# Gate and up projections with the tokens stationary and 512 weight columns moving

## The chip, the cores and the metric

The kernel runs on one core of one Trainium2 chip. The metric is the device time of one launch in microseconds. TensorE (PE, with its weight loads as PEld) multiplies, VectorE (DVE) and ScalarE (ACT) work elementwise and read and write PSUM, GpSimd (POOL) adds in SBUF, and SyncE (SP) issues the DMAs. Each engine works its own queue in order.

## The reference, cut to what matters

One layer for 512 tokens of width 2048, all in float32: token mixing, a residual, then the feed-forward part that the change touches.

```python
D_MODEL = 2048; SEQ = 512; D_FF = 5632

x = x + mix @ w_out[l]
h2 = _rms_norm(x, norm2_g[l])
x = x + (jax.nn.silu(h2 @ w_gate[l]) * (h2 @ w_up[l])) @ w_down[l]
```

## The kernel before, in words

**Stages.** Input projection with the two attentions and the convolution beside it (to about 394 us), output projection (to 582 us), gate and up (582 to 1441 us), down (to the end). Everything is emitted in one program order per engine (`manual_schedule`), so the order of the Python calls is the order of each engine's queue.

**Precision.** A float32 operand is split in two `fp32r` parts, a high part (a rounding copy) and a low part (what is left). A product is three matmuls: high by high, high by low, low by high.

**Strassen's scheme.** Gate, up and down are each computed as 2 by 2 block products with seven multiplications instead of eight (Winograd's form). A product is named by a number; `ORDER` (L66) gives the order for gate and up, `D_ORDER` (L76) that of down. The sums of the token operands are made once and kept in `ops[q, j]`, one tile of 128 x 512 for each of 7 products and 8 row pairs: 256 tokens' high parts in columns 0 to 255, their low parts in 256 to 511 (`TH` = 256). The sums of weight blocks are made on POOL (`sums`, called by `sums_now` at the start of a unit).

**Units.** Work on weights goes in units of 128 x 1024 float32. `pump` issues the DMA of a unit's raw block on SP as soon as its buffer was given back (`take`, `drop`), in the order of `entries`. `split_up_to` makes a unit's parts two units ahead (`SPLIT_AHEAD` = 2, three buffers each for `hi` and `lo`): ACT copies the raw block to `near` in PSUM and to `hi`, DVE subtracts `near` from the raw block into `lo`. `near` has two PSUM buffers (pool `high`). Units marked `"moves"` (those of down) have their columns permuted on the way, by the same three instructions (L280 to L282).

**Gate and up before.** There are 44 groups: for each pair `p` of 22 (one 128-row tile from each half of the feed-forward width) a gate group and an up group. A group has seven products, one unit each: `Block.multiply` (L1146) issues 8 matmuls with `wh` stationary and 512 columns moving (256 tokens' high and low parts side by side) and 8 with `wl` stationary and 256 columns moving (high parts). The features lie on the partitions of the result and the tokens on its columns; main and rest halves of a bank are added by DVE (`both`, `add`, `done`). `finish` multiplies by the token scale `R_21` (from `norm2a` and `norm2b`) and applies Silu for gate, and multiplies up by gate. Then `sums1`, `sums2` (POOL) form the operands of down, and `piece1` to `piece4` split them (ACT, DVE) and store them to `od`.

**Down.** `Down.product` (L1345) has the tokens' operands stationary (`acts`, read back from `od` by `load_next`) and 512 columns of `wh` and `wl` moving (L1404 to L1406), two banks, one for each 128 tokens.

**Queues of small work.** `later(n, fn)` puts a call into `evacs` (run at the start of a unit, before its splits are issued) or `extras` (run after its matmuls), n entries on. `done` of a product is run at the start of the unit behind it. Four PSUM banks (`outs`) take turns. `turn_x2` and `turn_x2_now` read the residual from DRAM turned (`z<-x2d`, in pieces of 32 floats), turn its 32 x 32 blocks on DVE and store them for down.

Of the kernel before, what the change touches and what calls it, by code (L numbers as in the profile page):

```python
# [65 lines left out]
ORDER = (5, 1, 7, 6, 2, 4, 3)  # L66
# [5 lines left out]
GU_ORDER = [*range(NP)]  # L72
# [7 lines left out]
LAID = (5, 7, 6, 4, 3, 1, 2)  # L80
# [36 lines left out]
def kernel(ctx: ExitStack, tc: tile.TileContext, xT, wi, wo, wgu, wd, cst_in, outT):  # L117
# [51 lines left out]
    def group(name, m, n, blocks):  # L169

        key = {k: (k, name) for k in ("11", "12", "21", "22", "s")}
        for k in ("22", "21", "11", "12"):
            entries.append((k + "ab"[m] if k[0] == "2" else k, key[k], blocks[k]))
        u = len(works)

        def add(to, a, b, last=None):
            def go():
                if to == a:
                    out = raws[key[to]][0]
                else:  # L180
                    out = take("s" + "ab"[m], key[to], n)
                nc.gpsimd.tensor_add(out[:, :n], raws[key[a]][0][:, :n], raws[key[b]][0][:, :n])  # L182
                if last:
                    drop(key[last])
            return go

        sums[u - 4].append(add("s", "21", "22"))
        sums[u - 3].append(add("21", "21", "11"))
        sums[u].append(add("s", "s", "11", "11"))
        sums[u + 2].append(add("s", "s", "12"))  # L190
        works.extend((key[k], last, None) for k, last in (
            ("s", False), ("11", False), ("21", True), ("s", False), ("12", True), ("22", True), ("s", True)))

    for p in GU_ORDER:
        for m in range(2):
            group(f"{'gu'[m]}{p}", m, 1024, {f"{i + 1}{k + 1}": [wgu[4 * (p + i * NP) + 2 * m + k]]
                                             for i in range(2) for k in range(2)})


    bufs = {"A": dict(zip(("21", "11", "s", "22"), ("21a", "22a", "sa", "22b"))),  # L200
            "B": dict(zip(("21", "11", "s", "22"), ("21b", "11", "12", "sb")))}

# [5 lines left out]
    for t, (g, r) in enumerate(DOWN):  # L208
# [12 lines left out]
        def add(c, out, one, other, buf=None):  # L221
            key, n = keys[c], size[c]

            def go():

                to = take(buf, key[out], n) if buf else raws[key[out]][0]
                nc.gpsimd.tensor_add(to[:, :n], raws[key[one]][0][:, :n], raws[key[other]][0][:, :n])
            return go
# [14 lines left out]
    def pump(limit, most=99):  # L243
        while at["entry"] < len(entries) and len(raws) < limit and entries[at["entry"]][0] not in held and most:
            most -= 1
            buf, key, parts = entries[at["entry"]]
            if len(parts[0].shape) == 3:
                n = 4 * parts[0].shape[-1]
                nc.sync.dma_start(take(buf, key, n)[:, :n].rearrange("p (n f) -> p n f", n=4), parts[0])
                at["entry"] += 1  # L250
                continue
            t, o = take(buf, key, sum(p.shape[-1] for p in parts)), 0
            for part in parts:
                nc.sync.dma_start(t[:, o:o + part.shape[-1]], part)
                o += part.shape[-1]
            at["entry"] += 1
# [830 lines left out]
    r2b = cp.tile([P, 3 * TH], F32, name="r2b")  # L1087
    R_12, R_21, R_1, R_2 = r2b[:, :T], r2b[:, TH:], r2b[:, :TH], r2b[:, TH:T]
# [4 lines left out]
    def norm2a():  # L1093

        n2["r"] = token_scale(ssum2, D, "n2", blk.banks[6][:, :NT])[1]
# [30 lines left out]
    class Block:  # L1126

        def __init__(self, name, m):  # L1130
            self.name = name

            self.banks = dict(zip((5, 1, 7, 6), outs))
            self.banks.update({3: self.banks[5], 4: self.banks[7], 2: self.banks[1]})
            outs[:] = [self.banks[q] for q in (6, 2, 4, 3)]

        def multiply(self, q, w, xs):
            wh, wl = w
            b = self.banks[q]
            at = [(x, slice(j * P, (j + 1) * P)) for j, x in enumerate(xs)]  # L1140

            begin = q in (5, 1, 6, 7)
            for low in ((0, 1) if flip[0] else (1, 0)):
                for x, s in at:
                    out, lhs, rhs = (b[:, TH:], wl, x[:, :TH]) if low else (b, wh, x)
                    nc.tensor.matmul(out, lhs[:, s], rhs, start=begin, stop=x is xs[-1] and low == flip[0],  # L1146
                                     skip_group_check=True)
                    begin = False
            flip[0] = 1 - flip[0]
            later(0, self.done, q)  # L1150

        def both(self, q, out):
            nc.vector.tensor_reduce(out, self.banks[q].rearrange("p (a b) -> p b a", a=2),
                                    axis=mybir.AxisListType.X, op=ALU.add)

        def add(self, q, out, first=None, sign=nc.vector.tensor_add):
            main, rest = halves(self.banks[q])
            sign(out, out if first is None else first, main)
            sign(out, out, rest)

    class Wide(Block):


        def __init__(self, p, m, gate):
            super().__init__(f"{'gu'[m]}{p}", m)
            self.p, self.gate = p, gate

        def done(self, q):
            if q == 1:
                self.u = slot(f"{self.name}u")  # L1170
                self.u1, self.u2 = halves(self.u)
                self.both(1, self.u1)
            elif q == 7:
                self.l, self.r = slot(f"{self.name}l"), slot(f"{self.name}r")
                self.both(7, self.r[:, :TH])
                self.add(5, self.r[:, :TH], sign=nc.vector.tensor_sub)
            elif q == 6:
                self.add(6, self.u2, self.u1)
                nc.gpsimd.tensor_sub(self.r[:, :TH], self.r[:, :TH], self.u2)
            elif q == 2:  # L1180
                self.both(2, self.r[:, TH:])
                self.finish(self.r, self.gate and self.gate.r)
            elif q == 4:
                c21 = self.l[:, TH:]
                main, rest = halves(self.banks[4])
                nc.vector.tensor_sub(c21, main, self.u2)
                nc.vector.tensor_add(c21, c21, rest)
            elif q == 3:
                self.add(3, self.l[:, :TH], self.u2)
                self.u = self.u1 = self.u2 = None  # L1190
                self.finish(self.l, self.gate and self.gate.l)
# [36 lines left out]
        def piece1(self):  # L1228
            self.piece(0, self.ta)
# [321 lines left out]
```

## Time and profile before

| | |
|---|---|
| median of 3 runs | 1867.45 us (1867.01 to 1867.95) |
| profiled execution | 1867.59 us, of which the span is 1865.9 us |
| granted TensorE clock | 1.00 |
| busy share of the span: PE, DVE, ACT, POOL | 100%, 78%, 71%, 61% |
| gate and up stage, by its first and down's first matmul | 581.93 to 1440.61 us |
| bytes moved, mean rate | 307.38 MB, 165 GB/s |

A row of a group names the line, the engine, the operation, output and inputs, shape and count, then busy time, the mean nanoseconds of one, and the idle time before it. In the timeline the first column is the start and the second the length, both in us; matmuls are pipelined, so the distance of two starts and not the length is what a matmul costs.

### The profile page before, as it was taken

The page shows a single profiled execution, that of the slowest core. Times are in us where ns is not written, and L with a number is a line of the kernel's source. Part 1 is how long each engine was busy: PE and PEld are TensorE (multiplying, and loading weights), DVE is VectorE, ACT ScalarE, POOL GpSimd, SP SyncE. Part 2 cuts the span into 40 slices and gives each one's busy share as a digit, 9 for nine tenths or more (in the row PEclk, how much of TensorE's full clock was granted, in tenths as well). Part 3 has the DMA queues.
Part 4 walks back from the last instruction along what each step waited for, and adds up shares of the span by engine and source line. Part 5 has one row for each costly group of instructions (what it writes and reads, how often), then busy time and mean ns, then how long its engine had stood idle before and what let it go on. Part 6 is the DMA issues. An engine that isn't in the chain of part 4 may idle for free.

```text
span 1865.9 us, 28280 instructions
## 1 busy us (share of the span) xinstructions
PE 1858.8 (100%) x9606; PEld 1591.2 (85%) x9606; DVE 1446.7 (78%) x2290; ACT 1330.5 (71%) x1840; POOL 1141.7 (61%) x828
## 2 busy tenths in 40 slices
PE   9999999999999999999999999999999999999998
PEld 7888888888888888888888888888888888888887
DVE  6778878998689777777777777777777777777777
ACT  6355644553457878888888888888888877778775
POOL 0125533100013877888878878788787878779775
PEclk9999999999999999999999999999999999999999
DMA  7243253343333455555555655555457867677645
GB/s 273 77 145 90 77 147 96 94 130 120 131 123 113 146 160 158 174 183 158 174 158 171 186 155 178 159 171 185 143 168 249 315 226 237 210 228 234 203 131 113
DMA packets 213328, 307.38 MB, mean 165 GB/s; under 512 B 75200, under 2 KB 124992, under 8 KB 213184
## 3 DMA queue, kind: packets, MB, share of 16 engines
q1 hardware_dynamic: 213040, 305.57, 52.3%
q8 instruction: 76, 1.25, 0.3%
q14 instruction: 68, 0.56, 0.1%
q10 hardware_dynamic: 144, 0.01, 0.0%
HBM read 244.03 MB, written 53.09 MB: 159 GB/s over the span
## 4 chain that ended last, share of the span: by engine, by line
PE 99%; DMA 0%; SPq 0%; DVE 0%; issue 0%; ACT 0%; DVEq 0%
PE out L1146 46%; PE out L1405 7%; PE out L1404 7%; PE out L1406 7%; PE o L317 3%; PE o L315 3%; PE o L316 3%; PE cq L315 2%; PE cq L317 2%; PE cq L316 2%; PE ak L315 1%; PE aq L315 1%; PE av L315 1%; PE aq L317 1%; PE aq L316 1%; PE av L316 1%
## 5 line engine op out<-in xcount | busy, mean ns | idle before, releaser
L1146 PE MATMUL out<-h,wh 128*128 128x512 f32 x2464 | 588.5, 391 | 0.0
L1146 PEld LDWEIGHTS out<-h,wh 128*128 128x128 f32 x2464 | 452.7, 188 | 87.5
L1146 PEld LDWEIGHTS out<-h,wl 128*128 128x128 f32 x2464 | 315.9, 191 | 12.0
L1146 PE MATMUL out<-h,wl 128*128 128x256 f32 x2464 | 319.6, 283 | 0.0
L1404 PE MATMUL out<-wh,a 128*128 128x512 f32 x620 | 240.4, 388 | 0.0
L1405 PE MATMUL out<-wl,a 128*128 128x512 f32 x620 | 240.3, 388 | 0.0
L1406 PE MATMUL out<-wh,a 128*128 128x512 f32 x620 | 240.3, 388 | 0.0
L286 ACT CAST wh<-w 128x1024 fp32r<-128x1024 f32 (+2 forms) x94 | 96.8, 1031 | 151.0 <-PE o L316 62.8
L264 DVE TENSOR_TENSOR wl<-w,wh 128x1024 fp32r<-128x1024 f32 (+2 forms) x95 | 113.2, 1191 | 41.1 <-ACT wh L286 39.5
L1404 PEld LDWEIGHTS out<-wh,a 128*128 128x128 f32 x620 | 116.4, 188 | 24.0
L1406 PEld LDWEIGHTS out<-wh,a 128*128 128x128 f32 x620 | 116.4, 188 | 23.8
L1405 PEld LDWEIGHTS out<-wl,a 128*128 128x128 f32 x620 | 116.4, 188 | 23.8
L1414 DVE TENSOR_TENSOR y<-y,out 128x512 f32<-128x512 f32 x164 | 106.2, 683 | 25.7 <-PE out L1406 23.8
L526 DVE SCALAR_TENSOR_TENSOR y<-bu,cst,y 128x511 f32<-128x511 f32 (+14 forms) x120 | 90.0, 750 | 0.7
L315 PE MATMUL o<-mh_c,wh 128*128 128x512 f32 x128 | 51.1, 399 | 0.0
L315 PE MATMUL cq<-hh,wh 128*128 128x512 f32 x128 | 50.5, 395 | 0.0
L317 PE MATMUL o<-mh_c,wl 128*128 128x512 f32 x128 | 50.0, 391 | 0.0
L316 PE MATMUL cq<-hl,wh 128*128 128x512 f32 x128 | 49.9, 390 | 0.0
L316 PE MATMUL o<-ml_c,wh 128*128 128x512 f32 x128 | 49.9, 390 | 0.0
L317 PE MATMUL cq<-hh,wl 128*128 128x512 f32 x128 | 49.9, 390 | 0.0
L431 POOL TENSOR_TENSOR lvr<-lvv,nhalf 128x4 f32<-128x4 f32 x1 | 1.9, 1923 | 70.7 <-DVE lvv L430 70.7
L182 POOL TENSOR_TENSOR w('s', 'g0')_5667<-w('21', 'g0')_5513,w('22', 'g0')_5511 128x1024 f32<-128x1024 f32 x1 | 2.5, 2454 | 69.0 <-DVE wl L264 69.0
(3062 smaller groups left out, 4941.6 us busy)
## 6 DMA issues: line engine op xcount, KB each, us to landing
od<-a SPq DMA_DIRECT2D x154, 256.0 KB, 4.7
a<-od SPq DMA_DIRECT2D x154, 256.0 KB, 5.5
w<-in_wi SPq DMA_DIRECT2D x58, 512.0 KB, 3.5
w<-in_wo SPq DMA_DIRECT2D x32, 512.0 KB, 3.5
x<-in_xT SPq DMA_DIRECT2D x16, 256.0 KB, 7.1
xr<-in_xT SPq DMA_DIRECT2D x16, 256.0 KB, 3.8
x2d<-xr SPq DMA_DIRECT2D x16, 256.0 KB, 2.0
z<-x2d SPq DMA_DIRECT2D x64, 64.0 KB, 3.8
```

Of the source, the lines that this page charges most:

```text
L182: nc.gpsimd.tensor_add(out[:, :n], raws[key[a]][0][:, :n], raws[key[b]][0][:, :n])
L264: fn(*args)
L286: (nc.vector.tensor_copy if u == 0 else nc.scalar.copy)(hi[:, :n], t[:, :n])
L315: nc.tensor.matmul(out, wh, xh, start=start, stop=False)
L316: nc.tensor.matmul(out, wh, xl, start=False, stop=False)
L317: nc.tensor.matmul(out, wl, xh, start=False, stop=stop)
L526: nc.vector.scalar_tensor_tensor(yconv[j][:, i:], hconv[j][:, :T - i], c, yconv[j][:, i:], op0=ALU.mult, op1=ALU.add)
L1146: nc.tensor.matmul(out, lhs[:, s], rhs, start=begin, stop=x is xs[-1] and low == flip[0], skip_group_check=True)
L1404: nc.tensor.matmul(b[:, lo:hi], x[:, high], wh[:, s], start=start, stop=False, skip_group_check=True)
L1405: nc.tensor.matmul(b[:, lo:hi], x[:, high], wl[:, s], start=False, stop=False, skip_group_check=True)
L1406: nc.tensor.matmul(b[:, lo:hi], x[:, low], wh[:, s], start=False, stop=last, skip_group_check=True)
L1414: getattr(eng, op)(t, t, src)
```

## The change

For gate and up the operands change places: 128 columns of `ops[q, j]` (128 tokens, high or low parts) become stationary, and 512 columns of `wh` or `wl` move (256 gate or up features from each of two pairs; two row pairs make a unit). A unit is then 12 matmuls of 512 columns, for two banks of 128 tokens. The 44 groups become 11 blocks of two halves (row pairs 0 to 3 and 4 to 7) of seven products of two units: 28 units a block, 308 units as before. The order of the products is new, and so are the weight buffers' turns; each raw block is read in two parts, in pieces of 1 KB instead of 4 KB.

Tokens lie on the partitions of the result. The first half's results are copied out of PSUM (`keep`, one bank on ACT, one on DVE), the others are added to them (`add`); the corrections by product 6 run on POOL. The token scale is now a per-partition scalar of Silu and of the multiplication `weigh`, so that the spread of the scale over the partitions goes. The result is turned to features on partitions: DVE turns 32 x 32 blocks (`turn`), `store` writes them to a tile in DRAM, and `Pair.read` reads them back, each time four DMAs of 32 partitions in pieces of 32 floats. `Pair` then makes the operands of down as before: sums on POOL, splits on ACT and DVE, stores to `od`. In the last block's second half two loads of down's operands are issued a unit (28 in all), where before three were in the last group (21 in all).

```diff
-ORDER = (5, 1, 7, 6, 2, 4, 3)
+ORDER = (7, 1, 4, 2, 5, 6, 3)
...
+def up_block(pair, m, half, j):
+    return [bass.AP(tensor=wgu.tensor, offset=wgu.offset + (4 * (pair + i * NP) + 2 * m + half) * P * 1024 + j * P,
+                    ap=[[1024, P], [4 * P * 1024, 2], [1, 2 * P]]) for i in range(2)]
...
+    for i, c in enumerate("AB"):
+        key = keys[c]
+        sums[base - 4 + i].append(plus(key["s"], key["21"], key["11"], 1024, bufs[c]["s"]))
+        sums[base + 2 + i].append(plus(key["21"], key["21"], key["22"], 1024))
+        sums[base + 6 + i].append(plus(key["11"], key["21"], key["11"], 1024))
+        sums[base + 7 + i].append(plus(key["12"], key["11"], key["12"], 1024))
+    works.extend((keys[c][k], last, "moves") for k, last in (
+        ("s", True), ("11", False), ("22", True), ("12", False), ("21", True), ("11", True), ("12", True)) for c in "AB")
...
-    def norm2b():
-        b = psum["high"].tile([P, 1024], F32, name="r2s", tag="h")[:, :T]
-        spread(n2["r"], "r2s", b)
-        nc.scalar.copy(R_12, b)
-        nc.scalar.copy(r2b[:, T:], b[:, :TH])
+    def norm2():
+        b = psum["high"].tile([P, 1024], F32, name="r2s", tag="h")[:, :NT]
+        n2["r"] = token_scale(ssum2, D, "n2", b)[1]
...
+    class Pair:
+        def __init__(self, dram, p, n):
+            for at, fn in ((0, self.read_l), (1, self.read_r), (4, self.sums), (5, self.piece_r), (7, self.piece_l),
+                           (8, self.sum4), (9, self.piece_a), (11, self.piece_4)):
+                later(at, fn, queue=extras)
+        def read(self, n, name):
+            t = slot(f"p{self.p}{name}")
+            for part in range(4):
+                at = (4 * n + part) * 32
+                nc.sync.dma_start(t[32 * part:32 * part + 32].rearrange("p (x i) -> p x i", i=32),
+                                  self.dram.rearrange("(x j) f -> j x f", j=32)[:, :, at:at + 32])
...
+        def sums(self):
+            nc.gpsimd.tensor_sub(n1, c11, c12)
+            nc.gpsimd.tensor_sub(c12, c12, c22)
+            nc.gpsimd.tensor_sub(n2, c12, c11)
...
+    class Up:
+        def product(self, q):
+            banks = outs[:2]
+            outs[:] = outs[2:] + banks
+            for c in range(2):
+                sums_now()
+                run(evacs)
+                wh, wl = next_unit()
+                for a, b in enumerate(banks):
+                    high, low = slice(a * P, (a + 1) * P), slice(TH + a * P, TH + (a + 1) * P)
+                    for f in range(2):
+                        x, s = ops[q, self.first + 2 * c + f], slice(f * T, (f + 1) * T)
+                        nc.tensor.matmul(b, x[:, high], wh[:, s], ...)
+                        nc.tensor.matmul(b, x[:, high], wl[:, s], ...)
+                        nc.tensor.matmul(b, x[:, low], wh[:, s], ...)
+                yield
+                run(extras)
+            later(0, self.done, self.first == 0, q, banks)
...
+        def done(self, first, q, banks):
...
+            if q == 6:
+                u = [self.c.pop((2, 0, a)) for a in range(2)]
+                for a in range(2):
+                    self.add(1, 0, a, u[a], nc.gpsimd, "tensor_sub")
+                for a in range(2):
+                    if first:
+                        self.c[0, 1, a] = u[a]
+                    else:
+                        self.add(0, 1, a, u[a], nc.gpsimd)
+                for a in range(2):
+                    self.add(1, 1, a, u[a], nc.gpsimd, "tensor_sub")
+            if not first and q in (2, 3):
...
+                later(0, self.gate, k, queue=extras)
+                at = 1 if k else 6
+                later(at, self.weigh, k)
+                later(at + 1, self.turn, k)
+                later(at + 2, self.store, k, queue=extras)
+            if not first and q == 3:
+                later(5, Pair, self.dram, 2 * self.n, 0, queue=extras)
+                later(15, Pair, self.dram, 2 * self.n + 1, 1, queue=extras)
...
-    for g in range(2 * NP):
-        p, m = GU_ORDER[g // 2], g % 2
-        blk = Wide(p, m, gate if m else None)
...
+    for n in range(NBLOCKS):
+        blk = Up(n)
+        for blk.first in (0, 4):
+            for i, q in enumerate(ORDER):
+                for c, _ in enumerate(blk.product(q)):
+                    at_unit = (7 if blk.first else 0) * 2 + 2 * i + c
+                    if n == 0 and at_unit == 2:
+                        norm2()
+                    if 1 <= n <= 8 and at_unit in (9, 12, 25, 27):
+                        (turn_x2 if at_unit % 16 == 9 else turn_x2_now)(SUMS[2 * n - 2 + at_unit // 16])
+                    if n == NBLOCKS - 1 and blk.first:
+                        load_next(2)
```

More of the change, by code (lines that the diff above doesn't have):

```diff
@@ L71 @@
 FEED = 46
-GU_ORDER = [*range(NP)]
+NBLOCKS = NP // 2
 D_ORDER = (7, 1, 5, 6, 4, 2, 3)
@@ L167 @@
         works.append((u, True, nc.vector))
[L169 to L192, printed above, removed]
@@ L221, in add @@
         def add(c, out, one, other, buf=None):
[L222 to L228, printed above, removed]
+            return plus(keys[c][out], keys[c][one], keys[c][other], size[c], buf)
         for i, c in enumerate("AB"):
@@ L246, in pump @@
             buf, key, parts = entries[at["entry"]]
[L247 to L255, printed above, removed]
+            size = [part.shape[-1] * (part.shape[1] if len(part.shape) == 3 else 1) for part in parts]
+            t, o = take(buf, key, sum(size)), 0
+            for part, n in zip(parts, size):
+                to = t[:, o:o + n]
+                nc.sync.dma_start(to.rearrange("p (n f) -> p n f", n=part.shape[1]) if len(part.shape) == 3 else to, part)
+                o += n
             at["entry"] += 1
@@ L1124, in later @@
         queue[n].append((fn, *args))
[L1126 to L1159, printed above, removed]
@@ L1459, in done @@
                     later(2 * n + 2, put, self.g, i, k, queue=extras)
-    blk = gate = None
     for t in range(len(DOWN)):
```

190 lines of the change are left out of this document (99 added, 91 removed).

## The prediction

> **What bounds the kernel now.** I read the page's busy shares and the chain of waits first, then TensorE's timeline in the two stages that use the two arrangements, then the other engines by stage.
>
> ```profile
> PE 1858.8 (100%) x9606; PEld 1591.2 (85%) x9606; DVE 1446.7 (78%) x2290; ACT 1330.5 (71%) x1840; POOL 1141.7 (61%) x828
> PEclk9999999999999999999999999999999999999999
> PE out L1146 46%; PE out L1405 7%; PE out L1404 7%; PE out L1406 7%; PE o L317 3%; PE o L315 3%; PE o L316 3%; PE cq L315 2%; PE cq L317 2%; PE cq L316 2%; PE ak L315 1%; PE aq L315 1%; PE av L315 1%; PE aq L317 1%; PE aq L316 1%; PE av L316 1%
> ```
>
> TensorE is busy for the whole span at full clock, and the chain that ends last is matmuls, 46% of it on L1146, the one line of gate and up. A busy PE need not be PE at its peak, so I look at the distance of the starts.
>
> ```profile
> 904.37 3.82 PE L1146 MATMUL out<-h,wh 128*128 128x512 f32 x16
> 908.02 2.08 PE L1146 MATMUL out<-h,wl 128*128 128x256 f32 x16
> 909.93 3.82 PE L1146 MATMUL out<-h,wh 128*128 128x512 f32 x16
> 913.59 2.08 PE L1146 MATMUL out<-h,wl 128*128 128x256 f32 x16
> 915.50 0.86 PE L1146 MATMUL out<-h,wh 128*128 128x512 f32 x3
> ...
> 1699.69 0.39 PE L1404 MATMUL out<-wh,a 128*128 128x512 f32 x1
> ...
> 1705.81 0.39 PE L1404 MATMUL out<-wh,a 128*128 128x512 f32 x1
> ```
>
> In gate and up, four units take 915.50 - 904.37 = 11.13 us, 2.7825 us a unit. Sixteen matmuls of 512 columns take 908.02 - 904.37 = 3.65 us (228.1 ns each), sixteen of 256 columns 909.93 - 908.02 = 1.91 us (119.4 ns): half the columns cost more than half the time. In down, with the tokens stationary and 512 columns moving, the 27 steps from the first to the last row shown (the rows left out are the matmuls between, one a step) take 6.12 us, 226.7 ns each. No wait shows between them.
>
> ```profile
> 581.93 1.98 PE L1146 MATMUL out<-h,wh 128*128 128x512 f32 x8
> 587.50 0.95 PE L358 MATMUL out<-ones,ssum 128*128 128x1 f32 x8
> 588.31 2.11 PE L1146 MATMUL out<-h,wh 128*128 128x512 f32 x8
> 594.01 0.60 PE L364 MATMUL r2s<-ident,n2r 128*128 128x128 f32 x4
> 594.36 2.09 PE L1146 MATMUL out<-h,wh 128*128 128x512 f32 x8
> 1440.61 0.39 PE L1404 MATMUL out<-wh,a 128*128 128x512 f32 x1
> ```
>
> The stage lasts 1440.61 - 581.93 = 858.68 us: 308 units of 2.7825 us are 857.0, the row sums of the norm (587.50 to 588.31) 0.81, the spread of the scale (594.01 to 594.36) 0.35, together 858.2. So the stage is TensorE's own pace, with half a microsecond of anything else.
>
> **The change, part by part.**
>
> *TensorE.* A unit becomes 12 matmuls of 512 columns. At down's 226.7 ns that is 2.720 us, 308 units 837.9 us; the row sums stay (0.81), the spread goes. 838.7 against 858.7: **-20.0 us**. The other bound is 512 columns at the 228.1 ns of the old stage: 2.737 us a unit, 843.0 + 0.8, -14.9 us. I take down's value, since its operands, order and accumulation are the new ones.
>
> [...]
>
> *Is there cover for the rest?* All other work must fit beside 2.720 us units, on engines that were this busy before:
>
> ```profile
> 900.00:1000.00 100.00, 100.00 (x577) 88.40 (x576) 76.63 (x114) 83.25 (x108) 80.63 (x52) 1.00 0.55 171
> ...
> L281 ACT CAST wh<-w('11', 'd0A')_14861 x3: 1055/1057/1057, 1440.9 to 1468.0; 128x1024 fp32r<-128x1024 f32 x3
> L280 ACT CAST wn<-w('11', 'd0A')_14861 x3: 1007/1010/1022, 1438.1 to 1466.4; 128x1024 fp32r<-128x1024 f32 x3
> L282 DVE TENSOR_TENSOR wl<-w('11', 'd1A')_15411,wn x3: 1214/1215/1222, 1479.5 to 1506.7; 128x1024 fp32r<-128x1024 f32 x3
> L1414 DVE TENSOR_TENSOR y<-y,out x164: 648/682/689, 1445.8 to 1849.4; 128x512 f32<-128x512 f32 x164
> L1424 ACT COPY d0u<-out x2: 581/585/589, 1451.1 to 1451.7; 128x512 f32<-128x512 f32 x2
> L1267 DVE STREAM_TRANSPOSE zt<-z x16: 703/704/705, 714.0 to 1298.5; 128x512 f32<-128x512 f32 x16
> L526 DVE SCALAR_TENSOR_TENSOR y<-bu,cst,y x120: 693/732/941, 62.7 to 460.4; 128x511 f32<-128x511 f32 x4, 128x510 f32<-128x510 f32 x4, 128x509 f32<-128x509 f32 x4, 128x508 f32<-128x508 f32 x4
> L1225 DVE TENSOR_TENSOR a<-u0r,u0n x2: 412/413/414, 626.5 to 626.8; 128x256 fp32r<-128x256 f32 x2
> L1414 POOL TENSOR_TENSOR y<-y,d0u x8: 1282/1300/1309, 1453.2 to 1488.0; 128x512 f32<-128x512 f32 x8
> L1208 POOL TENSOR_TENSOR u0ta<-u0r,u0l x1: 742/742/742, 624.9 to 624.9; 128x256 f32<-128x256 f32 x1
> 901.84 2.42 POOL L182 TENSOR_TENSOR w('s', 'u8')_9381<-w('21', 'u8')_9193,w('22', 'u8')_9191 128x1024 f32<-128x1024 f32 x1
> ```
>
> The first row is a window of the old stage: DVE, ACT and POOL 77, 83 and 81% busy, the DMA engines 55%. For a new block of 28 units (76.2 us):
> - DVE: 28 low parts at 1.215, 18 sums and 5 copies out of PSUM at 0.68, 4 multiplications at 0.73, 4 turns at 0.70, 14 splits at 0.41, some 2 turns of the residual: 62.6 us, 82%.
> - ACT: the splits stay (28 times 1.01 + 1.06), Silu and the splits of down's operands stay, 5 copies at 0.59 come: 2.9 us, +4%, and the unit is 2% shorter: about 89%.
> - POOL: 16 weight sums at 2.42, 10 corrections at 1.30, 8 sums at 0.74: 57.6 us, 76%.
>
> On average all fit. What counts is where the work piles up.
>
> *The start.*
>
> ```profile
> 588.22 0.42 DVE L1043 TENSOR_TENSOR h<-h,h 128x256 fp32r<-128x256 f32 x1
> 588.56 1.21 DVE L264 TENSOR_TENSOR wl<-w('21', 'g0')_5513,wn 128x1024 fp32r<-128x1024 f32 x1
> ```
>
> DVE makes the last token operands until 588.6. (Two neighbours of 0.42 us start 0.34 us apart: lengths overlap.) The third unit's low part, which stood behind them, is now issued with its split, ahead of them; so they end at 589.8, and the fourth unit's low part at 591.0, due at 581.93 + 3 x 2.72 + 0.23 = 590.3: **+0.7 us** (0 to 2). The token operands of rows 4 to 7 aren't needed before unit 14, so none of them is late.
>
> *The turn of a block*, the worst place, on DVE. Call 0 the start of the next block's first unit. The corrections by product 6 start on POOL when DVE has summed it, at -5.44 + 2 x 0.68 = -4.1; the fourth ends at +1.1. DVE's second sum of product 3 waits for it and ends at 1.8. Then, in queue order: the low part of unit 2 to 3.0 (due with that unit's second matmul, 5.7), two `weigh` to 4.5, unit 3 to 5.7 (due 8.4), two turns to 7.1, two `weigh` to 8.5, a copy to 9.2, unit 4 to 10.4 (due 11.1), two turns to 11.8, unit 5 to 13.0 (due 13.8). So 13 us of work go through a stretch of 10.9 us, and being two units ahead saves it by 0.7 us. I price it at 0 inside the stage, with 1.3 us a block as the other end (POOL 2 us behind at that point).
>
> *The hand-over to down* is that turn with four sums of product 7 in place of one copy: 3 x 0.68 = 2.0 us more against 0.7 us of room, and less than that, since neighbours overlap, as in the row pair above. I take **+0.8 us** (0 to 2).
>
> *SP and the turned reads.* A block adds 4 stores and 16 reads (some 0.5 us of SP each) and 16 weight DMAs, and the reads wait on SP for the stores to land. Behind them in SP's queue stand weight blocks, issued 10 us and more ahead of their use.
>
> ```profile
> 933.95 2.02 SPq L1263 DMA_DIRECT2D z<-x2d  x4
> L1263 SPq DMA_DIRECT2D z<-x2d x64: 369/487/1132, 700.2 to 1286.2; - x64
> DMA to landing us min/median/max: 3.3/3.8/5.2
> 934.00:939.00 5.00, 5.00 (x31) 4.43 (x31) 3.86 (x6) 4.70 (x7) 3.31 (x4) 1.00 0.69 157
> 1440.00:1500.00 60.00, 60.00 (x267) 49.67 (x266) 44.82 (x57) 49.10 (x59) 48.63 (x29) 1.00 0.90 318
> ```
>
> The read of the residual has the same shape and pieces: issue 2 us for four, 3.8 us (3.3 to 5.2) to landing. The next row is the stretch in which one set and one weight block (512 KB) moved: 0.69 x 5.0 = 3.5 us of all DMA engines, of which the block is 1.5 us at the rate of the last row, 318 / 0.90 = 353 GB/s. So a set (256 KB) costs some 2.0 us, four sets and four stores (0.75 us each) a block 11 us of 76: the DMA share goes from 0.55 to about 0.7. Enough is left; I price it at 0.
>
> **Sum** against the profiled execution (span 1865.9 us, its own time 1867.59, 0.14 above the median): -20.0 + 0.8 + 0.7 = -18.5 us. 1867.45 - 18.5 = **1849.0 us**, -1.0%. The likeliest case's own range is 1845.5 (no stall, and 1 us less than the sum) to 1854 (the 228.1 ns bound).
>
> **The rivals.**
>
> *DVE is late at every turn* (chance 0.15). For it: the 0.7 us of room, and that DVE there waits for POOL, which stands behind 2.42 us sums. Against it: that overlap, which I left out of the 13 us. Each 1 us beyond the room costs 11 us: at 0.4 to 1.3 us a block 1853 to 1863.
>
> *The turned reads land late, and POOL stands still* (chance 0.18, slower). In the second half of a block, `Pair.sums` stands in POOL's queue ahead of three weight sums. The read can be issued some 12 us into that half (behind a weight block that waits for unit 5's split) and lands at 16 to 18. From there two sums (1.5 us), two weight sums (4.8), a split (1.0 + 1.2) must be done by 30.1, when unit 11 starts: the read has until 21.6. Landing 3.6 us later than I assume, it costs 11 us for each further us; from 1.7 us on the gain is gone. At 7 us over the 3.8 us of the residual's read (twice as many reads queued, between stores and weights) it is 37 us: 1886 (1872 to 1900). For it: pieces of 128 bytes, and two sets at a time. Against it: 5.2 us as the longest of 64. [...]
>
> *TensorE's pace does not follow the shape* (chance 0.09): the change makes the products as it says, but a unit stays at 2.76 to 2.78 us, because what slows the old stage (a change of the moving operand every matmul, small waits) comes back in the new one. Then 308 units take 850 to 857 us, and with the start and the hand-over the time is 1861 to 1868, mostly within 0.2% of before. Against it: the two rates lie in the same trace, the better one with the new arrangement. [...]
>
> **How the numbers follow.** Forecast 0.58, late turns 0.15, late reads 0.18, no change 0.09. A measurement of this kernel can tell some 0.2% (3.7 us) from no change. Faster: 0.58 + 0.15 = 0.73; same 0.08; slower 0.19 (late reads, and a little of the third). The range takes in the forecast, the late turns and part of the unchanged: 1845.5 to 1868.
>
> **What would show it.** Right: starts 226.7 ns apart through the new stage, 838 to 840 us from its first matmul to down's. Late turns: gaps of TensorE once in 76 us, ended by DVE's low part. Late reads: POOL idle until a read of the turned tile lands, then TensorE waiting for a weight split. Wrong altogether: a unit over 2.78 us without gaps.

## The result, and the profile after

The changed kernel takes **1948.66 us** (median of 4, 1945.85 to 1949.01), the kernel before in the same comparison 1867.23 (1866.95 to 1867.95): a ratio of 1.0432, 95% interval 1.0418 to 1.0447. It is 4.3% slower, where the prediction had 1.0% faster. The profiled execution took 1949.01 us, its span 1947.3.

First the page of the changed kernel: the busy times, and the chain that ended last.

```profile
PE 1877.9 (96%) x8370; PEld 1542.3 (79%) x8370; DVE 1480.2 (76%) x2147; ACT 1365.2 (70%) x1893; POOL 1085.8 (56%) x762
PE 79%; DVE 7%; DMA 4%; SPq 3%; ACT 2%; POOL 2%; issue 2%; DVEq 0%; POOLq 0%; ACTq 0%
```

TensorE is no longer busy all the time, and DVE, DMA, SP, ACT and POOL now hold 18% of a chain in which matmuls led every line. The busy times of the other engines hardly rose: none of them is the new bound by its sum. Next the same kernel by stage: gate and up (from its first matmul to down's), down, and the 100 us of the old stage that the prediction looked at. Columns: length, busy time and count of PE, PEld, DVE, ACT and POOL, granted TensorE clock, DMA share, GB/s.

```profile
581.90:1506.60 924.70, 871.90 (x3706) 706.60 (x3706) 676.42 (x813) 738.60 (x945) 614.04 (x363) 0.97 0.65 176
1506.60:1947.30 440.70, 425.87 (x1865) 351.15 (x1863) 329.31 (x399) 324.65 (x386) 342.44 (x204) 0.98 0.68 213
900.00:1000.00 100.00, 94.50 (x401) 76.79 (x400) 72.25 (x88) 81.83 (x107) 70.34 (x44) 0.97 0.67 181
```

The stage takes 924.7 us instead of 858.7 (forecast 838.7), down 440.7 instead of 425.3. In the stage TensorE is idle for 924.70 - 871.90 = 52.8 us, and its clock is 0.97. TensorE's timeline of one block shows both.

```profile
1079.79 0.39 PE L1183 MATMUL out<-wl,h 128*128 128x512 f32 x1
1088.18 0.39 PE L1184 MATMUL out<-wh,h 128*128 128x512 f32 x1
1089.39 0.47 PE L1181 MATMUL out<-wh,h 128*128 128x512 f32 x1 [0.83 <-DVE b5c L1195]
1091.03 0.50 PE L1183 MATMUL out<-wl,h 128*128 128x512 f32 x1 [1.17 <-DVE wl L270]
1097.58 0.80 PE L1183 MATMUL out<-wl,h 128*128 128x512 f32 x1 [3.55 <-DVE wl L270]
1098.17 0.63 PE L1184 MATMUL out<-wh,h 128*128 128x512 f32 x1
...
1102.44 0.63 PE L1181 MATMUL out<-wh,h 128*128 128x512 f32 x1
```

From 1079.79 to 1088.18 (the first two rows; the ones between are left out) there are 37 steps in 8.39 us, 226.7 ns each: the new pace is what was forecast. Then come three gaps, two of them ended by a low part of the weights that DVE wrote late (L270), and after the longest, ten steps in 4.27 us, 427 ns each. The window right behind it has the clock:

```profile
1097.60:1102.80 5.20, 5.20 (x12) 4.12 (x13) 5.20 (x8) 3.54 (x5) 0.00 (x0) 0.50 0.01 3
```

What was DVE doing? DVE and POOL at that place, in order of time:

```profile
1087.63 0.71 DVE L1288 STREAM_TRANSPOSE zt<-z 128x512 f32<-128x512 f32 x1 [3.52 <-DMA z<-x2d]
1088.38 2.35 POOL L172 TENSOR_TENSOR w('21', 'u12A')_10049<-w('21', 'u12A')_10049,w('22', 'u12A')_10265 128x1024 f32<-128x1024 f32 x1
1090.70 2.39 POOL L172 TENSOR_TENSOR w('21', 'u12B')_10078<-w('21', 'u12B')_10078,w('22', 'u12B')_10291 128x1024 f32<-128x1024 f32 x1
1090.90 5.49 DVE L1252 SCALAR_TENSOR_TENSOR b5c<-b5c,n2r,b5c 128x512 f32<-128x512 f32 x2
1093.05 2.80 POOL L172 TENSOR_TENSOR w('11', 'u12A')_10153<-w('21', 'u12A')_10049,w('11', 'u12A')_10153 128x1024 f32<-128x1024 f32 x1
1096.32 1.21 DVE L270 TENSOR_TENSOR wl<-w('11', 'u12B')_10180,wn 128x1024 fp32r<-128x1024 f32 x1
```

Two things. DVE stands 3.52 us for a read of the residual (z), with everything behind it. Then the two multiplications of `weigh` take 5.49 us, more than two POOL sums long, and the low part that TensorE needs is queued behind them. The first is so at the eight turns that have a z (3.5 to 4.4 us each; the profile puts three of these waits down to the read of z and five to a weight block). The second is so in every block: the longest of the four weighings of a block is 2.84 to 2.89 us in all eleven. Two of the rows, the second from a block whose turn has no z (count, then min/median/max in ns):

```profile
L1252 DVE SCALAR_TENSOR_TENSOR b5c<-b5c,n2r,b5c x4: 703/1736/2837, 1090.9 to 1099.3; 128x512 f32<-128x512 f32 x4
L1252 DVE SCALAR_TENSOR_TENSOR b9c<-b9c,n2r,b9c x4: 739/2076/2886, 1427.2 to 1436.4; 128x512 f32<-128x512 f32 x4
```

Alone it takes 0.70 to 0.74 us (forecast 0.73), beside POOL's sums up to 2.89, and of the two sums beside it at 1090.90 the second is longer too (2.80 us, the first 2.39). Both inputs of `weigh` lie in SBUF, and so do those of the sums. My guess, which the first experiment tries, is that the two hold each other up there; two of the expectations name it the port. The rows show the lengths and not what makes them.

POOL, with the weight sums in its queue, also stands earlier in the block, at the two turned reads of a block's second set of products:

```profile
1058.84 0.74 POOL L1143 TENSOR_TENSOR p9a<-p9l 128x256 f32<-128x256 f32 x1 [4.75 <-DMA p9l<-bd]
1065.65 0.74 POOL L1144 TENSOR_TENSOR p9l<-p9l,p9r 128x256 f32<-128x256 f32 x1 [6.08 <-DMA p9r<-bd]
```

What each of these three costs, the profile alone does not say; the experiments take them apart.

### The profile page after: what moved, and what is told of

It reads as the page before. It is cut to its first block, busy times and chain, and to the rows that moved or that the text cites. A ratio compares the mean times of both kernels' runs of the same rounds, so it can differ in the third digit from the quotient of the medians.

```text
span 1947.3 us, 26413 instructions
## 1 busy us (share of the span) xinstructions
PE 1877.9 (96%) x8370; PEld 1542.3 (79%) x8370; DVE 1480.2 (76%) x2147; ACT 1365.2 (70%) x1893; POOL 1085.8 (56%) x762
## 4 chain that ended last, share of the span: by engine, by line
PE 79%; DVE 7%; DMA 4%; SPq 3%; ACT 2%; POOL 2%; issue 2%; DVEq 0%; POOLq 0%; ACTq 0%
PE out L1183 10%; PE out L1184 10%; PE out L1181 10%; PE out L1422 7%; PE out L1421 7%; PE out L1423 7%; PE o L305 3%; PE o L303 3%; PE o L304 3%; DVE wl L270 2%; PE cq L303 2%; PE cq L305 1%; PE cq L304 1%; SPq L1130 1%; ACT wh L269 1%
## 5 line engine op out<-in xcount | busy, mean ns | idle before, releaser
L1183 PE MATMUL out<-wl,h 128*128 128x512 f32 x1232 | 491.9, 399 | 40.0 <-DVE wl L270 39.6
L1181 PE MATMUL out<-wh,h 128*128 128x512 f32 x1232 | 488.9, 397 | 10.6 <-DVE b8c L1195 1.7
L1184 PE MATMUL out<-wh,h 128*128 128x512 f32 x1232 | 488.1, 396 | 0.0
L1183 PEld LDWEIGHTS out<-wl,h 128*128 128x128 f32 x1232 | 236.0, 192 | 100.7 <-DVE wl L270 51.5
L1181 PEld LDWEIGHTS out<-wh,h 128*128 128x128 f32 x1232 | 236.2, 192 | 66.4 <-issue 13.5
L1184 PEld LDWEIGHTS out<-wh,h 128*128 128x128 f32 x1232 | 236.4, 192 | 48.3
```

The costliest lines, as they stand in the source:

```text
L1181: nc.tensor.matmul(b, x[:, high], wh[:, s], start=c == f == 0 and q in (7, 1, 5, 6), stop=False, skip_group_check=True)
L1183: nc.tensor.matmul(b, x[:, high], wl[:, s], start=False, stop=False, skip_group_check=True)
L1184: nc.tensor.matmul(b, x[:, low], wh[:, s], start=False, stop=c == f == 1, skip_group_check=True)
```

## The experiments

Two pieces of the changed code, `later(n, f)` and the tables of units, decide at which unit a step is put into its engine's queue; most edits below move such a number. Each ratio is to the kernel before, run beside it on the same chip.

| | gate in | z | pairs | weighings | us | ratio, 95% interval |
|---|---|---|---|---|---|---|
| the change | SBUF | as is | as is | as is | 1948.66 | 1.0418 to 1.0447 |
| 1 | PSUM | as is | as is | as is | 1910.89 | 1.0219 to 1.0249 |
| 2 | SBUF | read earlier | as is | as is | 1978.04 | 1.0574 to 1.0609 |
| 3 | PSUM | read earlier | as is | as is | 1925.42 | 1.0295 to 1.0326 |
| 4 | PSUM | read earlier | last two sets later | as is | 1927.37 | 1.0304 to 1.0335 |
| 5 | PSUM | turned later | as is | as is | 1895.68 | 1.0135 to 1.0165 |
| 6 | PSUM | as is | sums later | as is | 1946.76 | 1.0414 to 1.0456 |
| 7 | PSUM | turned later | sums later | as is | 1941.85 | 1.0379 to 1.0414 |
| 8 | PSUM | turned later | 2nd set read earlier | as is | 1859.40 | 0.9949 to 0.9975 |
| 9 | PSUM | turned later | 2nd set read earlier | apart | 1856.07 | 0.9927 to 0.9957 |
| 10 | SBUF | turned later | 2nd set read earlier | apart | 1859.10 | 0.9940 to 0.9973 |
| 11 | SBUF | turned later | 2nd set read earlier | as is | 1898.67 | 1.0154 to 1.0184 |
| 12 | SBUF | as is | as is | apart | 1945.48 | 1.0396 to 1.0431 |

**1. The gate in PSUM.** One of `weigh`'s two inputs leaves SBUF, and Silu comes just ahead of it:

```
-                later(0, self.gate, k, queue=extras)
+                later(at - 1, self.gate, k, queue=extras)
...
-                g = self.c[0, k, a]
-                nc.scalar.activation(g, g, AF.Silu, scale=self.scale(k, a))
+                nc.scalar.activation(g[:, a * T:(a + 1) * T], self.c[0, k, a], AF.Silu, scale=self.scale(k, a))
```

> Silu of gate is written to PSUM instead of SBUF, and for k = 0 it runs just ahead of weigh, so that weigh (DVE) has one SBUF operand in place of two; all else as in the changed kernel. Theory A (weigh with two SBUF operands and POOL's sums, which read SBUF too, block each other: 0.70 us alone, up to 2.89 us beside a sum): all 44 weigh take 0.7 us, POOL's 2.8 us sums fall to 2.4, a turn costs TensorE some 2 us in place of 5 us of gaps, and there are fewer windows of half clock; 1865 to 1885 us. Theory B (DVE stands because the turned read of the residual lands late): the gaps of blocks 1 to 8 stay, only the turns behind blocks 0 and 9 improve; 1930 to 1940 us.

1910.89 us, 38 less than the change and between the two expectations. `weigh` is at its own length in every block (0.74 us at most), and the gap at the turn has another name (the first experiment's DVE, ACT and TensorE):

```profile
1070.46 0.71 DVE L1290 STREAM_TRANSPOSE zt<-z 128x512 f32<-128x512 f32 x1 [4.14 <-DMA z<-x2d]
1071.51 1.02 ACT L268 CAST wn<-w('11', 'u12A')_10163 128x1024 fp32r<-128x1024 f32 x1 [3.53 <-DVE a L1115]
1073.56 0.51 PE L1182 MATMUL out<-wh,h 128*128 128x512 f32 x1 [2.79 <-ACT wh L269]
1073.73 1.39 DVE L1253 SCALAR_TENSOR_TENSOR b5c<-b5c,n2r,g 128x512 f32<-128x512 f32 x2
```

Two weighings in 1.39 us beside the same POOL sums. DVE's wait for z now ends last: ACT needs a PSUM buffer that a piece on DVE, queued behind z, has to release.

**2, 3 and 4. z read earlier.** The reads of z go four units ahead; in 2 alone, in 3 with the gate in PSUM, in 4 also with the sums and pieces of the last two sets eight units later (for the hand-over into down).

```
-                    if 1 <= n <= 8 and at_unit in (9, 12, 25, 27):
+                    if 1 <= n <= 8 and at_unit in (5, 12, 21, 27):
```

> The reads of the residual (z) are issued four units earlier in each half (units 5 and 21 in place of 9 and 25), the turn of z stays where it is; weigh as in the changed kernel. Theory A (port): the 3.5 us wait of DVE for z goes, but weigh still takes up to 2.9 us and the turns behind blocks 1 to 8 look like the one behind block 9, which has no z (gaps of 1.0 and 3.4 us); some 1935 us (1925 to 1945). Theory B (late z): the gaps go; 1865 to 1885 us.

> Both edits together. Theory A: no gap left at the turns, hence no half clock in the stage; what remains over the forecast is the start and the hand-over to down, 10 to 15 us; 1855 to 1865 us. Theory B gives the same as with the earlier read alone, 1865 to 1885 us. If the pace itself were the fault the stage would stay over 900 us.

> Both edits, and for the last two pairs the sums and splits behind the turned reads run 8 units later, so that ACT does not stand for a read that lands late at the start of down (in the changed kernel 7.2 us, with 3.4 us of TensorE behind it and a window of half clock). If that wait is the rest of the loss: 5 to 10 us less than with both edits alone, 1848 to 1856 us. If the start of down is held by its own loads: the same as with both edits.

1978.04 and 1925.42 us, above what either theory had, and 1927.37: an earlier read made it 29 and 15 us worse. (Gate and up takes 903.8 us in 3, over the 900 that was to mean a slow pace; but its steps too are 226.7 ns apart between the gaps.) In the second experiment POOL, ACT and TensorE show a new gap in the middle of a block:

```profile
1083.05 0.73 POOL L1144 TENSOR_TENSOR p9l<-p9l,p9r 128x256 f32<-128x256 f32 x1 [6.66 <-DMA p9r<-bd]
1096.12 0.41 ACT L1114 CAST a<-p9l 128x256 fp32r<-128x256 f32 x1 [3.92 <-DMA od<-a]
1098.47 0.52 PE L1181 MATMUL out<-wh,h 128*128 128x512 f32 x1 [3.99 <-ACT wh L269]
```

POOL stands 6.66 us for a turned read of the products, so the split is late already; and the store of a piece (od), now behind z's reads in SP's queue (issued at 1092.47, the reads at 1090.29), releases its buffer 3.92 us late, with ACT's splits behind it. So the reads of z cannot be moved there. The hand-over is not what is left of the loss: 4 is as slow as 3, with down at 435.0 us instead of 436.8.

**5. z turned later.** The reads stay; DVE's two transposes go to unit 15 and to unit 3 of the next block.

```
+                    if 1 <= n <= 8 and at_unit in (9, 25):
+                        turn_x2(SUMS[2 * n - 2 + at_unit // 16])
+                    if 1 <= n <= 8 and at_unit == 15 or 2 <= n <= 9 and at_unit == 3:
+                        turn_x2_now(SUMS[2 * n - 2 if at_unit == 15 else 2 * n - 3])
```

> The gate in PSUM as in the first experiment, and in addition the two vector transposes of z are queued later (unit 15 instead of 12; unit 3 of the next block instead of 27), the reads of z stay where they are. In the first experiment VectorE stood 4.14 us at the second one, waiting for z, and ScalarE then stood 3.53 us for a piece that VectorE had behind it (1071.51), with a TensorE gap of 2.79 us. Theory (VectorE's place for z is too early): these 11 gaps (21.0 us in all) and most of the 32 us at half clock go, and the time falls from 1911 to about 1880 (1872 to 1892). Rival (GpSimd's six corrections, which end at 1070.6, hold the next weight sums in any case): the gap keeps its place under another name and the time stays at 1905 to 1915.

1895.68 us, 15 less than the first experiment, half of what the theory had. What remains in most blocks are two gaps of TensorE, one of 1.2 us for a low part of DVE and one of 0.6 to 1.7 us behind a wait of POOL (fifth experiment, POOL, ACT and TensorE):

```profile
1036.99 0.75 POOL L1143 TENSOR_TENSOR p9a<-p9l 128x256 f32<-128x256 f32 x1 [6.23 <-DMA p9l<-bd]
1043.34 0.73 POOL L1144 TENSOR_TENSOR p9l<-p9l,p9r 128x256 f32<-128x256 f32 x1 [5.60 <-DMA p9r<-bd]
1049.64 1.02 ACT L268 CAST wn<-w('11', 'u11B')_9814 128x1024 fp32r<-128x1024 f32 x1 [3.22 <-POOL w('11', 'u11B')_9814 L172]
1051.68 0.50 PE L1182 MATMUL out<-wh,h 128*128 128x512 f32 x1 [1.06 <-ACT wh L269]
```

Read from the bottom: TensorE waits for a split, the split for a weight sum of POOL, and POOL had stood 11.8 us at the two turned reads of the block's second set of products, with that sum behind it.

**6 and 7. The pairs' sums later.** Sums and pieces four units further behind their reads, without and with 5.

```
-            for at, fn in (... (4, self.sums), (5, self.piece_r), (7, self.piece_l), ...
+            for at, fn in (... (8, self.sums), (9, self.piece_r), (11, self.piece_l), ...
```

> The gate in PSUM as in the first experiment, and in addition GpSimd's sums of a pair and its pieces are queued four units later after the turned reads (8 to 15 units behind instead of 4 to 11); z is as in the change. GpSimd stood 4.84 and 5.79 us at the second pair's two reads (1041.33, 1047.87) with the weight sums behind it. Theory (the place in GpSimd's queue is too early for reads that land this late): these waits fall under 2 us each, the half-block after them is no longer late, and as VectorE's wait for z at the turn is untouched, the time falls only in part, to 1890 to 1908. Rival (the reads are slow because the DMA engines are full, and come as late against the new place): the waits keep 4 us and more and the time stays at 1905 or above.

> The gate in PSUM, z's transposes later and the pairs' sums later, together. If the four causes (the port of the weighting, z's place, the pairs' place, and the half clock that each gap brings) are all of the loss in this stage, the blocks come down to 28 units of 2.72 us (76.2 us) and the time to 1850 to 1868 (what is left over 1849 is the hand-over into the third stage). If the DMA engines' load of 0.67 is itself a limit, gaps remain at other places and it stays at 1880 or above.

1946.76 and 1941.85 us, 36 and 46 worse than without. Both theories failed on the time. POOL does not stand at the second set's reads any more in either run, as the theory of 6 had it; the time went past 1905 as its rival had it, but not for the rival's reason. The second set's pieces now fall into the turn of the block, which is the likely cause; no run tests it by itself. In the seventh experiment's waits one line of TensorE stops in 30 places for ACT; the row of ACT, which stands 4.84 us for the store of an earlier piece, lies 2 us ahead of one of them:

```profile
PE out L1182 <- ACT wh L269: 30.0, 30, 2.7
1068.26 0.41 ACT L1114 CAST a<-p8a 128x256 fp32r<-128x256 f32 x1 [4.84 <-DMA od<-a]
```

More distance between read and use takes POOL's wait away, but a later use costs more than that wait did.

**8. The second set read earlier.** Its reads three units ahead, its sums and pieces at their old units:

```
-                later(15, Pair, self.dram, 2 * self.n + 1, 1, queue=extras)
+                later(12, Pair, self.dram, 2 * self.n + 1, 1, 3, queue=extras)
```

(the last argument is added to the units of everything behind the reads).

> The fifth experiment (gate in PSUM, z's transposes late), and the turned reads of each second pair are issued three units earlier, while GpSimd's sums and the pieces keep their places. In the fifth experiment GpSimd still stood 6.23 and 5.60 us at that pair's two reads, and some 8 us later TensorE had a gap of 0.55 to 1.67 us for a split (ACT wh L269) whose weights GpSimd had summed late. Theory (the distance from read to sum is too short, and there is room for the reads earlier): GpSimd's waits there fall below 2 us each, the gap goes, a block falls from 80.0 to about 78.2 us and the time from 1896 to 1872 to 1882. Rival (a read earlier in SyncE's queue delays the stores and weights behind it, as z's reads did when they were moved ahead in the second experiment): the gap only moves, 1890 or above.

1859.40 us, 36 less than the fifth and 0.4% under the kernel before. POOL no longer waits for these reads:

```profile
1017.82 0.74 POOL L1143 TENSOR_TENSOR p9a<-p9l 128x256 f32<-128x256 f32 x1 [0.38 <-DMA od<-a]
1018.64 0.74 POOL L1144 TENSOR_TENSOR p9l<-p9l,p9r 128x256 f32<-128x256 f32 x1
```

It came out 13 us better than the low end of the expectation, since the gap that I had put down to the crowded turn (1.2 us at DVE's low part) went as well. Nothing at the turn itself was changed, so that gap too hung on POOL's lateness.

**9 and 10. The weighings apart, and then the gate back in SBUF.** The first weighing one unit earlier, the second one later; in 10 the gate is written in place again, which is the only difference.

```
-                at = 1 if k else 6
+                at = 2 if k else 5
```

> As the run before it, and the weighting of the first half of the rows comes one unit earlier and that of the second one unit later, so that two weightings, two turns and two hand-overs do not fall into the same two units. In the fifth experiment VectorE had 1.30 + 1.36 + 0.68 + 1.21 + 1.30 us in a row from 1069.17 to 1073.40 ahead of a split, and TensorE a gap of 1.2 us once per block there. Theory (VectorE's place at the turn is the last stall): that gap goes as well, blocks come to 76.2 to 76.8 us and the time to 1850 to 1862, under the 1867 of before. Rival (VectorE is simply short of time at the turn): a gap of about 1 us appears at a neighbouring unit and the time stays at 1870 or above.

> The run before it with one thing undone: the gate is written in place in SBUF again, so that the weighting has two SBUF inputs as in the change. Theory (VectorE's weighting stands while GpSimd works on SBUF): it takes up to 2.8 us instead of 0.74, TensorE stands 3 to 4 us once per block with a window of half clock behind it, and the time is 30 to 60 us above the run before it. Rival (with the weightings four units apart there is room for the wait): within 10 us of the run before it.

1856.07 us, the lowest median of all; and 1859.10. Against the eighth, the ninth's interval overlaps: what the weighings apart bring there is not resolved. The ninth's time is in its expected range, but the gap that it was to remove had gone in the eighth already, so that is no support for its theory. By stage, the ninth:

```profile
581.90:1425.20 843.30, 841.03 (x3707) 696.34 (x3706) 639.84 (x814) 740.63 (x944) 611.87 (x364) 1.00 0.72 193
1425.20:1853.50 428.30, 421.11 (x1865) 347.72 (x1863) 321.95 (x399) 324.16 (x387) 339.78 (x203) 1.00 0.70 219
```

The tenth is the surprise: I expected 30 to 60 us for the gate in SBUF and got 3, with overlapping intervals; its rival had it. The weighings are still stretched (the tenth's DVE, two of `weigh` each):

```profile
1044.70 2.48 DVE L1253 SCALAR_TENSOR_TENSOR b5c<-b5c,n2r,b5c 128x512 f32<-128x512 f32 x2
1053.48 3.18 DVE L1253 SCALAR_TENSOR_TENSOR b5c<-b5c,n2r,b5c 128x512 f32<-128x512 f32 x2
```

2.48 and 3.18 us instead of 1.4, but the first pair now stands beside POOL's corrections (six in 8.49 us), the second beside one weight sum, and TensorE has no gap there. The stall is hidden, not gone.

**11 and 12. One half of the cure each.** The change with the waits moved alone (z turned later, second set read earlier), and with the weighings apart alone (Silu just ahead of each, as in 10).

> The change with two places in the queues moved and nothing else: z's transposes later, the second pair's turned reads three units earlier. The gate is in SBUF and the weighting at its own place, as in the change. It differs from the run before it (1859) only in the place of gate and weighting. Theory (two SBUF inputs against GpSimd, in a place with no room): the weightings again take up to 2.8 us, TensorE again waits 3 to 4 us for a split of VectorE once per block with a window of half clock behind it, and the time is 1895 to 1925. Rival (what cost was the waits for transfers alone; the weighting's stall is covered once these are gone): 1860 to 1875.

> The change with the other thing moved alone: weightings four units apart with the gate just ahead of each, the gate in SBUF; z's transposes and the pairs' reads as in the change. Theory (the waits for transfers are a cause of their own): VectorE stands about 4 us for z at the turn and GpSimd 10 us and more at the second pair's reads, TensorE's gaps for ACT wh stay, and the time is 1890 to 1930. Rival (the crowded turn was all of it): 1860 to 1875.

1898.67 us, in the expected range, and 1945.48, above it. In the eleventh nine of the stage's turns have one gap left, of 2.6 us, where `weigh` stands ahead of the low part. Below are the weighings ahead of one of them, five of the nine rows of TensorE, and one step behind the fourth:

```profile
1066.73 3.57 DVE L1252 SCALAR_TENSOR_TENSOR b5c<-b5c,n2r,b5c 128x512 f32<-128x512 f32 x2
833.17 0.50 PE L1183 MATMUL out<-wl,h 128*128 128x512 f32 x1 [2.61 <-DVE wl L270]
913.90 0.50 PE L1183 MATMUL out<-wl,h 128*128 128x512 f32 x1 [2.62 <-DVE wl L270]
993.00 0.50 PE L1183 MATMUL out<-wl,h 128*128 128x512 f32 x1 [2.62 <-DVE wl L270]
1072.08 0.50 PE L1183 MATMUL out<-wl,h 128*128 128x512 f32 x1 [2.62 <-DVE wl L270]
1074.11 0.63 PE L1184 MATMUL out<-wh,h 128*128 128x512 f32 x1
1074.54 0.63 PE L1181 MATMUL out<-wh,h 128*128 128x512 f32 x1
1152.73 0.50 PE L1183 MATMUL out<-wl,h 128*128 128x512 f32 x1 [2.59 <-DVE wl L270]
```

In the twelfth DVE first stands, 2.31 us ahead of z's transpose, and then meets POOL's weight sums with its weighings, so that TensorE waits 6.21 us for a bank that DVE empties behind them (DVE, POOL, then TensorE):

```profile
1090.55 0.71 DVE L1288 STREAM_TRANSPOSE zt<-z 128x512 f32<-128x512 f32 x1 [2.31 <-DMA w('12', 'u12A')_10331<-in_wgu]
1091.49 5.45 DVE L1252 SCALAR_TENSOR_TENSOR b5c<-b5c,n2r,b5c 128x512 f32<-128x512 f32 x2
1093.60 2.79 POOL L172 TENSOR_TENSOR w('21', 'u12B')_10078<-w('21', 'u12B')_10078,w('22', 'u12B')_10289 128x1024 f32<-128x1024 f32 x1
1097.68 0.77 PE L1181 MATMUL out<-wh,h 128*128 128x512 f32 x1 [6.21 <-DVE b5c L1195]
```

At the turns of blocks 0 and 9, which have no z, the twelfth has no such gap (none, and 0.35 and 1.17 us), and its longest weighing there is 2.5 us, as in the tenth, instead of 2.8.

Whether the causes add up depends on the cure. With the gate in PSUM they do: 38 us by itself (1), 50 for moving the waits by itself (11), 89 together (8). Setting the weighings apart is worth 3 us by itself (12) and 40 with the waits moved (11 to 10): this cure works only once the waits are out of the way, z's above all by those two turns.

## Why the prediction was wrong, by its own steps

- **TensorE's pace: right.** 226.7 ns a step, and in the ninth experiment the whole stage at 843.3 us against 838.7 forecast. "TensorE's pace does not follow shape" is out.
- **The turn of a block: the step that failed.** It was priced at 0, with two `weigh` at 0.73 us each; here two took 5.49 us beside POOL's sums of weights, and with the gate in PSUM the time is 38 us lower (39 from 11 to 8). The 0.73 was the median of a row of 120, from a stage without sums of weights: most of them had no POOL instruction beside them, and the longest, 0.94 us, had two. The row was the right instruction in the wrong company. The kernel before gave a hint that I passed over: where DVE works beside POOL, in splits and sums, one of its inputs is in PSUM (a low part takes 1.21 to 1.22 us beside a weight sum and 1.20 to 1.22 with none), and the multiplications of `finish` are POOL's own. The rival "DVE is late at every turn" (0.15) had the sign, a gap for DVE's low part once a block, but neither the size nor the reason.
- **What was left out of that queue.** z's transpose was counted among DVE's busy times, but it was not put into the queue of the turn, and its wait of 3.5 us for the read was not seen; turning z later was worth 15 us (1 to 5). The read lands later than before, at a median of 4.9 us instead of 3.8:

```profile
z<-x2d SPq DMA_DIRECT2D x64, 64.0 KB, 4.9
```

- **The turned reads: the other term that was put at 0.** The rival had their place right, with 0.18 and 1872 to 1900 us. POOL did stand at the second set's reads, 10.8 us in the changed kernel and 11.8 in the fifth experiment, and the eighth shows that place alone to be worth 36 us. The rival's limit, a release 21.6 us into the half, was right too: in the block shown of the changed kernel the second read releases POOL at 21.3 us (1065.65, the half from 1044.3) and TensorE has no gap at unit 11; in the fifth experiment it is 22.8 us (1043.34, the half from 1020.5), and the gap there is the 1.06 us in the row at 1051.68. Its price was short: 1.2 us late for 11 blocks would be 13 us and not 36, since POOL's lateness went on into the turn, where nine gaps of 1.2 us went with it in the eighth. Both rivals came together, which no case of mine had: 1949 lies beyond both.
- **The sum.** From 1948.66 the gate in PSUM takes 38 us, z turned later 15, the second set read earlier 36, in that order: 1859.40. That is 89 of the 100 us between forecast and measurement.
- **The clock: not priced at all.** In the stage, idle time is 50.5 us more than in the ninth experiment (52.8 against 2.3), and TensorE's busy time is 30.9 us more (871.90 against 841.03) for the same matmuls: the granted clock is 0.97 against 1.00, and 0.50 over the 5.2 us behind the 3.55 us gap shown above. Of 81.4 us, 38% is this. It is part of what the cures above are worth, not one more term.
- **DMA share: right, and harmless as a share.** 0.67 against the forecast's 0.7; the ninth experiment runs the stage at 0.72 with no gap behind its start. When a read was issued, and what stood behind it, counted.
- **The hand-over: +0.8 us forecast, +15.4 measured** (440.7 against 425.3). Its rows in the changed kernel:

```profile
1523.41 0.77 PE L1421 MATMUL out<-wh,a 128*128 128x512 f32 x1 [5.21 <-issue]
1555.03 0.59 ACT L1110 CAST p20n<-p20r 128x512 fp32r<-128x512 f32 x1 [7.20 <-DMA p20r<-bd]
1558.21 0.80 PE L1421 MATMUL out<-wh,a 128*128 128x512 f32 x1 [3.36 <-ACT wh L269]
```

  The first gap, 5 us, is there only where `weigh` is as in the change (also in 2 and 11, not with the gate in PSUM or the weighings apart). The second stands behind a turned read (p20r) that ACT waits for. In the ninth experiment 3.0 us of the hand-over's 15.4 are left.
- **The start: +0.7 forecast, a gap of 2.2 us measured**, and 2.2 to 2.5 in every experiment; DVE ended the fourth unit's low part at 592.4 us and not at 591.0. It is a small miss of the same kind: DVE's queue was priced too short.

With its forecast of 1849.0 the prediction described something near the kernel of the ninth experiment (1856.07), not this one: TensorE's term was right, and what was put at 0 beside it was not. Between the forecast and the ninth's profiled execution (1855.17) 6.2 us are left: 843.3 against 838.7 + 0.7 in the stage, 3.9, and 428.3 against 425.3 + 0.8 in down, 2.2. What stays open: by how much each of the two waits (z, second set) counts in the change by itself with the gate in SBUF, since they were moved together there; and what makes a later use (6 and 7) cost so much.

## What to carry to other kernels

Price an instruction by a row where the same neighbours run and the operands lie in the same memories, not by any row of its kind: beside POOL's sums `weigh` took up to 2.89 us with both inputs in SBUF and 0.74 us at most with one in PSUM (first experiment). When a step waits for a transfer in an in-order queue, look at what stands behind it, and try to give it distance by issuing the transfer earlier where the issuing queue has room: here that gained 36 us for one read and lost 15 to 29 for another, and a later use lost 36 to 46. A cure can look worthless while another fault stands ahead of it: setting the weighings apart showed 3 us alone and 40 once the waits were moved.

## What the runs showed of the hardware

- `weigh` with both inputs in SBUF, in the changed kernel: 0.70 to 0.74 us alone, 2.84 to 2.89 for the longest of each block beside POOL's sums of weights; with one input in PSUM, in the first experiment, 1.39 us for two beside the same sums.
- Half clock after gaps: behind the gap of 3.55 us in the changed kernel the granted clock was 0.50 for 5.2 us, with 427 ns a step. In the eleventh experiment the same gap of 2.6 us was followed by 427 ns steps at three of the nine turns (granted clock 0.79 over the 8 us from the gap's end) and not at the others (1.00 behind the gap at 1152.73). Blocks without it are 79.1 us long (913.90 to 993.00), blocks with it 80.7 (833.17 to 913.90, 1072.08 to 1152.73). What decides between the two, the runs do not show.
